# A hybrid layer's head loop with TensorE's order written by hand, and the step-size columns joined to the values' product

## The chip, the cores and the metric

The kernel runs on one core of one Trainium2 chip. The metric is device time in microseconds of one execution. The kernel before took 1650.42 us, the median of 3 runs (1649.81 to 1650.58).

## The reference, cut to what matters

A transformer block (pooled mixer with sparse attention, memory cross-attention, gated feed-forward) is followed by two hybrid layers over 512 tokens of width 1024. Only the hybrid layers are touched. One of them computes, from its input `x`:

```
proj = x @ w_in            # q, k, v, z_attn, z_ssm, xbc, dt_raw (16 columns, one for each state-space head)
attn = sliding_window_attention(q, k, v, sinks) * silu(z_attn)
xs, B, C = split(silu(causal_depthwise_conv(xbc)))         # 1024 + 256 + 256 channels
dt = softplus(dt_raw + dt_bias);  a = -exp(a_log)
y  = ssd_chunked(xs, dt, a, B, C) + xs * d_skip            # 4 chunks of 128 tokens
ssm = gated_rmsnorm(y, z_ssm)
out = layer_norm(alpha * x + concat(attn, ssm) @ w_out)
```

In `ssd_chunked`, with `a_cs` the running sum of `dt * a` inside a chunk, the diagonal part of a head is `(C B^T * exp(a_cs[l] - a_cs[s]) for l >= s) @ (xs * dt)`. The off-diagonal part multiplies `C` by a state that is carried from chunk to chunk and scales with `exp(a_cs[l])`.

## The kernel before, in words

Activations lie transposed: 128 channels on the partitions, 512 tokens along the free axis. A projection of 128 output channels is a *unit*: 1024 x 128 weights, loaded by one DMA into `wraw` and split into a rounded part `whi` (ScalarE, line 107) and the rest `wlo` (VectorE, two halves, line 110). The layer's input `h` is split in the same way. `mm3` (lines 147 to 154) then issues 24 matmuls of 512 columns: for each of 8 blocks `whi*xh` and `whi*xl`, then 8 times `wlo*xh`. There are three buffers each of `wraw`, `whi` and `wlo`. PSUM has 4 banks with the tag `mm` (units), 2 with `lg` and 2 with `tr`. Large tiles of 128 x 512 come from two pools of 34, `G` and `R`, and small ones from `ht`, `sq` and `rs` of two each.

SyncE's queue runs in the order of the program text. On the other engines a planner orders instructions at build time, by the text's order as priority and by its own estimate of when each could start. Once built, every engine runs its list in order.

One hybrid layer (`hybrid`) does this, in text order:

1. Four gate units (`z_ssm`), block by block over the two halves of the tokens (`units_by_k`, lines 174 to 177).
2. `dt`: 16 matmuls with a 48-column stationary tile, the columns of the high and the low part (line 931). Then the units of B and C with their convolution (`conv`, lines 895 to 906: one ScalarE operation, three on VectorE, tanh, one more on VectorE). The softplus, the scan over tokens and the exponentials of `dt` run on 16 partitions x 512 (lines 932 to 953). `a_cs` and its exponential go to DRAM; eight transposes (lines 959, 960) bring `dt` and `a_cs` to token order.
3. Convolution units 0 and 1, the products `C B^T` (line 979), units 2, 3 and 4.
4. `tokens(0)`: for each chunk four transposes (line 1007), two multiplications on VectorE (lines 1010, 1014) and the state's matmul (line 1016), whose result is added to the carried state (lines 1021, 1022).
5. The loop over eight pairs of heads. Step j issues one more unit (convolutions 5 to 7, then gates 4 to 7), `decay(j + 1)` and `heads(j)`; step 3 also issues `tokens(1)`. `decay` turns rows of `a_cs`, fetched from DRAM by broadcast, into weights: four clamped differences of 128 x 128 for each head, the exponential, and a product with `C B^T` on GpSimd or VectorE. The clamps run on ScalarE as a Relu (line 1057), or, for the first head of the pair from pair 3 on, on VectorE (line 1055). `heads` issues 16 matmuls (line 1070) and 6 (line 1076), and three VectorE operations (lines 1078 to 1080). Then the gate is multiplied in (line 1110) and squares are summed. Step 6 also issues the first half's norm (`gated_norm`, line 1087).
6. After the loop: the two key units; the values' product, 96 matmuls of 256 columns with `h` as the stationary operand (lines 1139 to 1141); the second half's norm; 16 heads of attention with the remaining query and gate units between them; the output projection with its tail.

Of the kernel before, what the change touches and what calls it, by code (L numbers as in the profile page):

```python
# [61 lines left out]
class Kern:  # L62
# [79 lines left out]
    def mm3(self, out, w, xs, m=P, start=True, stop=True, woff=0):  # L142

        nc = self.nc
        whi, wlo = w
        n = len(xs)
        for k, (xh, xl) in enumerate(xs):
            c = slice(woff + k * m, woff + (k + 1) * m)
            nc.tensor.matmul(out, whi[:, c], xh, start=start and k == 0, stop=False)  # L149
            nc.tensor.matmul(out, whi[:, c], xl, start=False, stop=False)  # L150
        self.begin()
        for k, (xh, xl) in enumerate(xs):
            c = slice(woff + k * m, woff + (k + 1) * m)
            nc.tensor.matmul(out, wlo[:, c], xh, start=False, stop=stop and k == n - 1)  # L154

# [719 lines left out]
    def l2_consts(self):  # L875
# [4 lines left out]
        self.small = self.load("small16", [16, 4], nc.sync)  # L880

    def hybrid(self, L):
# [4 lines left out]
        e16 = lambda: self.f("G")[:16, :]  # L887
        xr, e, uu, sm, dtf, acs, seg = (e16() for _ in range(7))
        nc.scalar.dma_start(seg, a["segs"])

# [4 lines left out]
        def conv(j, tag, w=None):  # L895

            y, o = self.f("ht"), self.f(tag)
            cw = lambda w: cwh[:, w * 12 + j : w * 12 + j + 1]
            pt = self.proj(W[4 + j], h, w=w)
# [14 lines left out]
        wd = self.s("w256", (P, 256), 9)[:, :P]  # L914
        nc.sync.dma_start(wd, a["w_dt"][L])
        wdt = self.s("wdt", (P, 48 * KD), 1, F32R)
        nc.gpsimd.memset(wdt.bitcast(F32), 0.0)
        w3, wd3 = wdt.rearrange("p (k m) -> p k m", m=48), wd.rearrange("p (k m) -> p k m", m=16)
        self.split(wd3, w3[:, :, :16], w3[:, :, 32:])

# [11 lines left out]
        nc.scalar.activation(xr, pt[32:48], AF.Identity, bias=self.small[:, L : L + 1])  # L932
        nc.vector.tensor_tensor(xr, pt[:16], xr, ALU.add)
        BC = [conv(8 + j, "R") for j in range(4)]
# [9 lines left out]
        nc.vector.scalar_tensor_tensor(dtf, xr, 0.0, uu, ALU.max, ALU.add)  # L944
        av = self.s("av", (16, 1), 2)
        nc.scalar.activation(av, self.small[:, 2 + L : 3 + L], AF.Exp)
        nc.vector.tensor_scalar(av, av, -1.0, None, ALU.mult)
        nc.vector.tensor_scalar(e, dtf, av, None, ALU.mult)
        nc.vector.tensor_tensor_scan(acs, seg, e, 0.0, ALU.mult, ALU.add)
        self.acsd = self.dp.tile([2, 16, S], F32, tag=f"acs{L}", name=f"acs{L}")  # L950
        nc.scalar.dma_start(self.acsd[0], acs)
        nc.scalar.activation(seg, acs, AF.Exp)
        nc.scalar.dma_start(self.acsd[1], seg)
        B, C = BC[:2], BC[2:]

        ptd = self.ps("tr")
        for c in range(4):
            cc = slice(c * P, (c + 1) * P)
            nc.tensor.transpose(ptd[:, c * 16 : c * 16 + 16], dtf[:, cc], self.ident[:16, :16])
            nc.tensor.transpose(ptd[:, 64 + c * 16 : 80 + c * 16], acs[:, cc], self.ident[:16, :16])  # L960
        dtt = self.s("dtt", (P, 128))
        nc.vector.tensor_copy(dtt, ptd[:, :128])
        dtok, atok = dtt[:, :64], dtt[:, 64:]
# [7 lines left out]
        nc.vector.tensor_tensor(dend, dend, dtok, ALU.mult)  # L971
        xs = [conv(0, "G"), conv(1, "G")]
# [28 lines left out]
        def tokens(g):  # L1001

            for c in range(4):
                cc = slice(c * P, (c + 1) * P)
                ptx = self.ps("tr")
                for j in range(4):
                    nc.tensor.transpose(ptx[:, j * P : (j + 1) * P], xs[4 * g + j][:, cc], self.ident)
                xdt[g, c] = self.f("G")
                o = c * 16 + 8 * g
                nc.vector.tensor_tensor(d3(xdt[g, c]), d3(ptx), bc(dtok, o), ALU.mult)  # L1010
                if c == 3:
                    break
                xe = self.f("ht")
                nc.vector.tensor_tensor(d3(xe), d3(ptx), bc(dend, o), ALU.mult)
                pst = self.ps("lg")
                nc.tensor.matmul(pst, bt[c][:, g * P : (g + 1) * P], xe, start=True, stop=True)
                prev = self.f("R")
                if c == 0:
                    nc.scalar.copy(prev, pst)
                else:  # L1020
                    nc.vector.tensor_tensor(d3(prev), d3(prevs[g, c - 1]), bc(cdec, o), ALU.mult)
                    nc.vector.tensor_tensor(prev, prev, pst, ALU.add)
                prevs[g, c] = prev

        def decay_rows(j):

            dfs, ee = [self.f("R") for _ in range(2)], self.f("R")
            for e_, df in enumerate(dfs):
                row = self.acsd[:, 2 * j + e_, :]
                nc.sync.dma_start(df, row[:1].broadcast_to([P, S]))  # L1030
                nc.sync.dma_start(ee[64 * e_ : 64 * e_ + 64, P:], row[1:, P:].broadcast_to([64, S - P]))
            return dfs, ee

        for j in range(2, 4):
            xs.append(conv(j, "G"))
        xs.append(conv(4, "G"))

        fill = [9, 10, 11, 28, 29, 30, 31]
        wn = self.weights(W[fill[0]])
        rows = [decay_rows(0), decay_rows(1)]  # L1040
        tokens(0)

        def decay(j):

            dfs, ee = rows.pop(0)
            if j < 6:
                rows.append(decay_rows(j + 2))
            for e_, df in enumerate(dfs):
                hd = 2 * j + e_
                cut = e_ == 0 and j >= 3  # L1050
                for c in range(4):
                    cc = slice(c * P, (c + 1) * P)
                    at = atok[:, c * 16 + hd : c * 16 + hd + 1]
                    if cut:
                        nc.vector.tensor_scalar(df[:, cc], df[:, cc], at, 0.0, ALU.subtract, ALU.min)
                    else:
                        nc.scalar.activation(df[:, cc], df[:, cc], AF.Relu, bias=at, scale=-1.0)
                nc.scalar.activation(df, df, AF.Exp, scale=1.0 if cut else -1.0)
# [31 lines left out]

        cat = [None] * 16
        accs = []
        ws = decay(0)
        for j in range(8):
            g = j // 4
            w = wn
            if j < 6:
                wn = self.weights(W[fill[j + 1]])
            if j < 3:
                xs.append(conv(5 + j, "G", w))  # L1100
            elif j < 7:
                zs.append(self.f("R"))
                silu(zs[-1], self.proj(None, h, w=w))
            nxt = decay(j + 1) if j < 7 else None
            if j == 3:
                tokens(1)
            heads(j, *ws)
# [321 lines left out]
```

## Time and profile before

| | |
|---|---|
| median of 3 runs | 1650.42 us (1649.81 to 1650.58) |
| the profiled execution's own time | 1650.6 us |
| its span, first to last instruction | 1648.8 us |
| busy: TensorE, VectorE, ScalarE, GpSimd | 97%, 69%, 49%, 13% of the span |
| mean granted TensorE clock | 0.994 of 2.4 GHz |

Times of stretches are microseconds from the span's start. The first hybrid layer's part that is touched goes from its gate units (about 836) to the start of attention (about 1010), the second's from about 1243 to about 1420. A matmul's duration in the rows runs from its start to the modelled arrival of its last result, so neighbours overlap; from one start to the next is what it costs the engine. "PE" is the matmuls, "PEld" the loading of the stationary operand, DVE is VectorE, ACT is ScalarE, POOL is GpSimd.

### The profile page before, as it was taken

How to read it: one execution, taken by the hardware profiler on the slowest of the kernel's cores; microseconds unless marked ns; L12 is line 12 of the kernel's file. 1: busy time of each engine (PE TensorE's matmuls, PEld its weight loads, DVE VectorE, ACT ScalarE, POOL GpSimd, SP SyncE). 2: the span in 40 equal slices, each digit the busy share in tenths (PEclk: the TensorE clock that was granted, in tenths of full speed). 3: DMA queues.
4: the chain of work that ended last, by engine and by line, in shares of the span. 5: the costliest groups of instructions: out<-in, count | busy, mean ns of one | idle time of the engine just before them, and what ended most of it. 6: DMA issues, size and time to landing. Idle time of an engine off the chain costs nothing. (4 is left out here: it accounts for less than half of the span.)

```text
span 1648.8 us, 24498 instructions
## 1 busy us (share of the span) xinstructions
PE 1601.2 (97%) x9014; PEld 1358.7 (82%) x9014; DVE 1140.7 (69%) x2490; ACT 805.5 (49%) x1571; POOL 212.4 (13%) x251
## 2 busy tenths in 40 slices
PE   8999999999999999999999999999999989999996
PEld 5778888889898888888998778887998867888786
DVE  6779967547886455533767998765497799777447
ACT  4543245336863333323556556665355555666424
POOL 2000213000100000000000121211230022111131
PEclk9999999999999999999999999999999999999998
DMA  6522332243233323234636223211452522322133
GB/s 222 198 97 76 120 103 64 77 158 116 81 116 111 102 92 100 89 104 119 196 124 191 80 77 103 78 65 51 141 171 81 178 87 78 102 78 65 64 103 116
DMA packets 66233, 180.28 MB, mean 109 GB/s; under 512 B 7953, under 2 KB 19169, under 8 KB 66113
## 3 DMA queue, kind: packets, MB, share of 16 engines
q1 hardware_dynamic: 56320, 166.75, 31.8%
q10 hardware_dynamic: 9792, 11.96, 2.4%
q8 instruction: 71, 1.16, 0.3%
q14 instruction: 50, 0.40, 0.1%
HBM read 170.14 MB, written 9.06 MB: 109 GB/s over the span
## 5 line engine op out<-in xcount | busy, mean ns | idle before, releaser
L149 PE MATMUL psmm<-G,whi 128*128 128x512 f32 (+2 forms) x1244 | 479.2, 388 | 2.2 <-ACT whi L107 2.2
L110 DVE TENSOR_TENSOR wlo<-wraw,whi 128x512 fp32r<-128x512 f32 x515 | 358.8, 718 | 174.8 <-ACT whi L107 123.8
L150 PE MATMUL psmm<-G,whi 128*128 128x512 f32 (+2 forms) x1244 | 473.6, 384 | 0.0
L107 ACT CAST whi<-wraw 128x1024 fp32r<-128x1024 f32 (+3 forms) x262 | 267.7, 1024 | 339.7 <-PE psmm L150 272.3
L154 PE MATMUL psmm<-G,wlo 128*128 128x512 f32 (+2 forms) x1244 | 299.5, 382 | 0.0
L149 PEld LDWEIGHTS psmm<-G,whi 128*128 128x128 f32 (+1 forms) x1244 | 233.3, 188 | 50.3 <-issue 3.5
L150 PEld LDWEIGHTS psmm<-G,whi 128*128 128x128 f32 (+1 forms) x1244 | 233.2, 188 | 45.3 <-issue 1.5
L154 PEld LDWEIGHTS psmm<-G,wlo 128*128 128x128 f32 (+1 forms) x1244 | 228.2, 187 | 45.0
L149 PE MATMUL psmm<-R,whi 128*128 128x256 f32 (+1 forms) x684 | 210.4, 329 | 0.0
L150 PE MATMUL psmm<-R,whi 128*128 128x256 f32 (+1 forms) x684 | 210.1, 328 | 0.0
L149 PEld LDWEIGHTS psmm<-R,whi 128*128 128x128 f32 x684 | 130.0, 190 | 11.8 <-issue 0.3
L150 PEld LDWEIGHTS psmm<-R,whi 128*128 128x128 f32 x684 | 130.0, 190 | 11.5
L154 PE MATMUL psmm<-R,wlo 128*128 128x256 f32 (+1 forms) x684 | 130.3, 329 | 0.0
L154 PEld LDWEIGHTS psmm<-R,wlo 128*128 128x128 f32 x684 | 106.2, 190 | 11.5
L200 POOL TENSOR_TENSOR acc<-acc,sq 128x512 f32<-128x512 f32 (+1 forms) x42 | 53.0, 1261 | 475.4 <-ACT sq L199 475.3
L1176 ACT ACTIVATE w<-w,st 128x256 f32<-128x256 f32 (+1 forms) x128 | 59.9, 470 | 29.3 <-DVE st L1174 29.3
L211 ACT ACTIVATE sq<-ht 128x512 f32<-128x512 f32 (+1 forms) x48 | 29.4, 613 | 60.8 <-DVE ht L902 30.0
L902 DVE SCALAR_TENSOR_TENSOR ht<-psmm,cwh,ht 128x511 f32<-128x511 f32 (+2 forms) x72 | 53.4, 742 | 5.8 <-ACT ht L900 4.6
L836 DVE TENSOR_TENSOR sq<-psmm,G 128x512 f32<-128x512 f32 (+1 forms) x24 | 15.5, 646 | 56.0 <-PE psmm L154 56.0
L1172 DVE CUSTOM_DVE_ANT_0 w<-pslg,w,sinks 128x256 f32<-128x256 f32 (+1 forms) x128 | 51.5, 444 | 1.1 <-PE pslg L1167 0.6
L199 ACT ACTIVATE sq<-G 128x256 f32<-128x256 f32 (+1 forms) x76 | 35.1, 463 | 34.3 <-DVE G L1264 25.9
L1181 POOL TENSOR_SCALAR w<-w,st 128x256 f32<-128x256 f32 x64 | 37.9, 604 | 86.8 <-DVE st L1179 79.0
(332 smaller groups left out, 2597.3 us busy)
## 6 DMA issues: line engine op xcount, KB each, us to landing
wraw<-w_in SPq DMA_DIRECT2D x112, 512.0 KB, 3.4
wraw<-w_out SPq DMA_DIRECT2D x56, 512.0 KB, 3.8
wraw<-w_down SPq DMA_DIRECT2D x24, 512.0 KB, 3.5
wraw<-w_gate SPq DMA_DIRECT2D x22, 512.0 KB, 3.4
wraw<-w_up SPq DMA_DIRECT2D x22, 512.0 KB, 3.4
R<-acs SPq DMA_DIRECT2D x32, 256.0 KB, 5.7
wraw<-w_down SPq DMA_DIRECT2D x12, 384.0 KB, 3.7
wraw<-w_proj_attn SPq DMA_DIRECT2D x8, 512.0 KB, 3.4
```

The lines of the kernel that those rows point to most:

```text
L107: nc.scalar.copy(hi[:, :n], raw[:, :n])
L110: nc.vector.tensor_tensor(lo[:, c], raw[:, c], hi[:, c].bitcast(F32), ALU.subtract)
L149: nc.tensor.matmul(out, whi[:, c], xh, start=start and k == 0, stop=False)
L150: nc.tensor.matmul(out, whi[:, c], xl, start=False, stop=False)
L154: nc.tensor.matmul(out, wlo[:, c], xh, start=False, stop=stop and k == n - 1)
L199: self.last_sq = nc.scalar.activation(t, src, AF.Square)
L200: (eng or nc.gpsimd).tensor_tensor(acc, acc, t, ALU.add)
L211: self.last_tanh = self.nc.scalar.activation(out, src, AF.Tanh, scale=scale)
L902: nc.vector.scalar_tensor_tensor(y[:, s:], pt[:, : S - s], cw(3 - s), y[:, s:], ALU.mult, ALU.add)
L1172: nc.vector.tensor_tensor_reduce(pr, pt, al[:, 256 - n :], 1.0, sink, ALU.add, ALU.max, mx[:, b : b + 1])
L1176: nc.scalar.activation(prs[b], prs[b], AF.Exp, bias=nm[:, b : b + 1], accum_out=sm[:, b : b + 1])
L1181: (nc.gpsimd if b % 2 else nc.vector).tensor_scalar(prs[b], prs[b], rc[:, b : b + 1], 1.0, ALU.mult, ALU.mult)
```

## The change

The `dt` columns are appended to the values' weights (272 columns), and this product moves to the place of the `dt` product, with four `mm` banks. Its values go to two tiles of the pool `R` (they were in `G`). `dt` now comes out with tokens on the partitions, so the softplus chain works on 128 x 64, and the running sum is a matmul with a triangular matrix. `a_cs` goes to DRAM as 64 rows of 128. B's and C's units come after this chain in the text. All clamps run on ScalarE. The loop becomes one block in which TensorE's instructions keep the text's order: nine units (convolutions 4 to 7, gates 4 to 7, the first key unit) are cut into single matmuls, 216 in all, and dealt out between the transposes, states and heads. `tokens` is split into `tokens(g, c)` and `state(g, c)`, and the scaled copies `xe` use the tag `rs` instead of `ht`.

```diff
+    def unit(self, w, xs):
+        whi, wlo = w
+        pt = self.ps()
+        def products():
+            n = len(xs)
+            for p in range(3 * n):
+                k = p // 2 if p < 2 * n else p - 2 * n
+                c = slice(k * P, (k + 1) * P)
+                lhs, rhs = (whi, xs[k][p % 2]) if p < 2 * n else (wlo, xs[k][0])
+                self.nc.tensor.matmul(pt, lhs[:, c], rhs, start=p == 0, stop=p == 3 * n - 1)
+                yield
+        return pt, products()
...
-        pt = self.ps("lg")[:48]
-        for k in range(KD):
-            for n, x in enumerate(h[k]):
-                nc.tensor.matmul(pt, wdt[:, 48 * k : 48 * k + 48], x, start=k + n == 0, stop=k == 7 and n == 1)
+        vs = [self.f("R") for _ in range(2)]
+        pv = [self.ps() for _ in range(4)]
+        for c in range(3):
+            n = min(3, KD - 3 * c)
+            wh, wl = self.weights(a["w_vdt"][L][:, 816 * c : 816 * c + 272 * n], 272 * n)
+            for t, pt in enumerate(pv):
+                o, tt = pt[:, :272], slice(t * P, (t + 1) * P)
+                for kk in range(n):
+                    k = 3 * c + kk
+                    ws = slice(272 * kk, 272 * kk + 272)
+                    nc.tensor.matmul(o, h[k][0][:, tt], wh[:, ws], start=k == 0, stop=False)
+                    nc.tensor.matmul(o, h[k][0][:, tt], wl[:, ws], start=False, stop=False)
+                    nc.tensor.matmul(o, h[k][1][:, tt], wh[:, ws], start=False, stop=k == 7)
...
+        for t, pt in enumerate(pv):
+            nc.vector.tensor_tensor(xr[:, 16 * t : 16 * t + 16], pt[:, 256:272], self.dtb[:, hb], ALU.add)
+            nc.scalar.copy(vs[t // 2][:, 256 * (t % 2) : 256 * (t % 2) + 256], pt[:, :256])
...
+        pa = self.ps("tr")
+        nc.tensor.matmul(pa[:, :64], self.tril, e, start=True, stop=True)
+        nc.vector.tensor_copy(atok, pa[:, :64])
+        prow = self.ps("tr")
+        nc.tensor.transpose(prow[:64, :P], atok, self.ident)
...
+        BC = [conv(8 + j, "R") for j in range(4)]
...
-                    if cut:
-                        nc.vector.tensor_scalar(df[:, cc], df[:, cc], at, 0.0, ALU.subtract, ALU.min)
-                    else:
-                        nc.scalar.activation(df[:, cc], df[:, cc], AF.Relu, bias=at, scale=-1.0)
+                    nc.scalar.activation(df[:, cc], df[:, cc], AF.Relu, bias=at, scale=-1.0)
...
+        def step(j):
+            if j < 7:
+                ws.append(decay(j + 1))
+            heads(j, *ws.pop(0))
+            if j < 5:
+                rows.append(decay_rows(j + 3))
...
+        with self.tc.manual_schedule(engines={mybir.EngineType.PE}):
+            for g, lead in ((0, 20), (1, 20)):
+                feed(lead)
+                tokens(g, 0)
+                tokens(g, 1)
+                feed(10 - 2 * g)
+                state(g, 0)
+                tokens(g, 2)
+                feed(6)
+                state(g, 1)
+                tokens(g, 3)
+                feed(8 - 2 * g)
+                state(g, 2)
+                if g == 0:
+                    for n, j in ((8, 0), (24, 1), (22, 2)):
+                        feed(n)
+                        step(j)
+                else:
+                    for n, j in ((0, 3), (10, 4), (22, 5), (22, 6), (22, 7)):
+                        feed(n)
+                        step(j)
+                    feed(2)
+        keys(self.proj(W[1], h))
```

## Rows read from the trace of the kernel before

**Rows 1.** The page: the engines' busy time, then TensorE's busy tenths in 40 slices of the span.

```profile
PE 1601.2 (97%) x9014; PEld 1358.7 (82%) x9014; DVE 1140.7 (69%) x2490; ACT 805.5 (49%) x1571; POOL 212.4 (13%) x251
...
PE   8999999999999999999999999999999989999996
```

**Rows 2.** Busy time by stretch: length, then each engine's busy microseconds (with the number of instructions), the granted clock as a share of 2.4 GHz, the DMA engines' busy share and GB/s. In the first hybrid layer: from the `dt` product to the first transposes of `tokens(0)`, from there to the values' product, that product, the start of attention, attention; then the second layer's stretch from its `tokens(0)` to its values' product.

```profile
854.60:910.90 56.30, 56.30 (x266) 45.67 (x266) 44.55 (x72) 34.98 (x62) 3.01 (x3) 1.00 0.59 172
910.90:993.60 82.70, 75.84 (x440) 58.18 (x439) 77.43 (x130) 44.13 (x81) 20.34 (x13) 1.00 0.26 79
993.60:1005.20 11.60, 11.60 (x98) 11.60 (x97) 7.13 (x12) 4.97 (x7) 0.00 (x0) 1.00 0.60 166
1005.20:1020.00 14.80, 14.45 (x69) 11.22 (x68) 12.86 (x25) 9.61 (x14) 0.00 (x0) 1.00 0.19 66
1020.00:1100.00 80.00, 80.00 (x461) 66.69 (x461) 59.40 (x182) 54.58 (x150) 17.46 (x32) 1.00 0.22 73
...
1315.50:1398.00 82.50, 76.00 (x441) 58.33 (x440) 77.55 (x128) 43.44 (x80) 19.15 (x13) 1.00 0.25 77
```

**Rows 3.** Who TensorE waited for between 836 and 1010: microseconds in total, times, the longest.

```profile
PE pslg L1016 <- DVE ht L1014: 3.1, 2, 1.9
PE pstr L1007 <- DVE G L905: 1.6, 1, 1.6
PE pstr L1070 <- DVE G L1078: 1.2, 2, 0.9
...
PE pstr L206 <- DVE G L1078: 0.5, 1, 0.5
```

**Rows 4.** TensorE in order of time (start, microseconds, engine, line): the `dt` product and the matmul that follows it; the first two of the eight small transposes; eight matmuls of a unit.

```profile
854.65 3.87 PE L931 MATMUL pslg<-G,wdt 128*48 128x512 f32 x16
...
858.36 0.39 PE L149 MATMUL psmm<-G,whi 128*128 128x512 f32 x1
...
880.24 0.23 PE L959 MATMUL pstr<-ident,G 16*128 16x16 f32 x1
880.32 0.21 PE L960 MATMUL pstr<-ident,G 16*128 16x16 f32 x1
...
991.74 1.98 PE L154 MATMUL psmm<-G,wlo 128*128 128x512 f32 x8
```

**Rows 5.** Groups of matmuls, shapes kept apart (count, busy microseconds, mean nanoseconds of one): the values' product, and one line that has a shape of 384 columns.

```profile
L1139 PE MATMUL psmm<-whi,G 128*128 128x256 f32 x64 | 18.1, 283 | 0.0
...
L594 PE MATMUL psmm<-G,G 128*128 128x384 f32 x8 | 2.7, 339 | 0.0
```

**Rows 6.** The end of the gate units in order of time, on ScalarE and VectorE: the next weights' split, and a gate's two operations between the halves of `wlo`.

```profile
853.65 1.05 ACT L107 CAST whi<-wraw 128x1024 fp32r<-128x1024 f32 x1 [7.47 <-PE psmm L176]
...
854.73 0.69 DVE L110 TENSOR_TENSOR wlo<-wraw,whi 128x512 fp32r<-128x512 f32 x1 [8.10 <-PE psmm L176]
...
855.34 0.74 DVE L911 SCALAR_TENSOR_TENSOR R<-R,psmm 128x256 f32<-128x256 f32 x2
856.00 0.68 DVE L110 TENSOR_TENSOR wlo<-wraw,whi 128x512 fp32r<-128x512 f32 x1
```

**Rows 7.** The softplus chain in order of time: the table load ahead of the logarithm and the logarithm; later, a small operation of 128 x 64.

```profile
863.28 1.28 ACT L940 ACT_TABLE_LOAD   x1
...
864.58 0.63 ACT L940 ACTIVATE G<-G 16x512 f32<-16x512 f32 x1
...
882.41 0.21 DVE L969 TENSOR_TENSOR dend<-pstr,dtt 128x64 f32<-128x64 f32 x1
```

**Rows 8.** TensorE in the loop, in order of time: a state's two passes and the transposes behind them, then one pair's 16 and 6 matmuls and what follows.

```profile
917.04 1.06 PE L1016 MATMUL pslg<-ht,G 128*128 128x512 f32 x2
917.94 0.49 PE L1007 MATMUL pstr<-ident,G 128*128 128x128 f32 x3
...
958.81 1.09 PE L1070 MATMUL pstr<-R,G 128*64 128x128 f32 x16
...
960.52 2.09 PE L154 MATMUL psmm<-G,wlo 128*128 128x512 f32 x8
```

**Rows 9.** VectorE in the loop, in order of time: two operations of a chunk's tokens, then a convolution's and a pair's.

```profile
920.51 0.68 DVE L1010 TENSOR_TENSOR G<-pstr,dtt 128x512 f32<-128x512 f32 x1
921.11 0.68 DVE L1014 TENSOR_TENSOR ht<-pstr,dend 128x512 f32<-128x512 f32 x1
...
923.67 0.74 DVE L902 SCALAR_TENSOR_TENSOR ht<-psmm,cwh,ht 128x511 f32<-128x511 f32 x1
924.34 0.74 DVE L1078 SCALAR_TENSOR_TENSOR G<-G,vecs,pstr 128x512 f32<-128x512 f32 x1
```

**Rows 10.** GpSimd's product and a clamp on VectorE in order of time, and an ordinary clamp shortly before them.

```profile
935.22 0.28 DVE L1055 TENSOR_SCALAR R<-R,dtt 128x128 f32<-128x128 f32 x1
...
936.18 1.30 POOL L1059 TENSOR_TENSOR R<-R,R 128x512 f32<-128x512 f32 x1 [12.06 <-ACT R L1058]
936.28 1.28 DVE L1055 TENSOR_SCALAR R<-R,dtt 128x128 f32<-128x128 f32 x1
```

**Rows 11.** The clamps between 919 and 1000, by line (count, busy microseconds, mean nanoseconds): on VectorE, and on ScalarE.

```profile
L1055 DVE TENSOR_SCALAR R<-R,dtt 128x128 f32<-128x128 f32 x20 | 8.3, 439 | 0.0
...
L1057 ACT ACTIVATE R<-R,dtt 128x128 f32<-128x128 f32 x28 | 9.2, 389 | 0.0
```

**Rows 12.** DMA issues: count, KB each, median microseconds from issue to landing.

```profile
R<-acs SPq DMA_DIRECT2D x32, 256.0 KB, 5.7
```

More of the change, by code (lines that the diff above doesn't have):

```diff
@@ L943, in hybrid @@
         nc.vector.tensor_tensor(uu, uu, sm, ALU.add)
[L944 to L963, printed above, removed]
+        nc.vector.scalar_tensor_tensor(dtok, xr, 0.0, uu, ALU.max, ALU.add)
+        av = self.s("av", (P, 16), 2)
+        nc.scalar.activation(av, self.alog[:, hb], AF.Exp)
+        d4 = lambda t: t.rearrange("p (c h) -> p c h", h=16)
+        nc.vector.scalar_tensor_tensor(d4(e), d4(dtok), -1.0, av.unsqueeze(1).broadcast_to([P, 4, 16]), ALU.mult, ALU.mult)
+        pa = self.ps("tr")
[3 more added lines that the diff above has]
+        nc.tensor.transpose(prow[:64, :P], atok, self.ident)
+        ar, er = self.s("ar", (64, P)), self.s("er", (64, P))
+        nc.scalar.copy(ar, prow[:64, :P])
+        nc.scalar.activation(er, prow[:64, :P], AF.Exp)
+        self.acsd = self.dp.tile([2, 64, P], F32, tag=f"acs{L}", name=f"acs{L}")
+        nc.scalar.dma_start(self.acsd[0], ar)
+        nc.scalar.dma_start(self.acsd[1], er)
         pl = self.ps("tr")
@@ L999, in hybrid, with tokens @@
         prevs = {}
[L1001 to L1019, printed above, removed]
-                else:
-                    nc.vector.tensor_tensor(d3(prev), d3(prevs[g, c - 1]), bc(cdec, o), ALU.mult)
-                    nc.vector.tensor_tensor(prev, prev, pst, ALU.add)
-                prevs[g, c] = prev
+        def tokens(g, c):
+            cc = slice(c * P, (c + 1) * P)
+            ptx = self.ps("tr")
+            for j in range(4):
+                nc.tensor.transpose(ptx[:, j * P : (j + 1) * P], xs[4 * g + j][:, cc], self.ident)
+            xdt[g, c] = self.f("G")
+            o = c * 16 + 8 * g
+            nc.vector.tensor_tensor(d3(xdt[g, c]), d3(ptx), bc(dtok, o), ALU.mult)
+            if c < 3:
+                xe[c] = self.f("rs")
+                nc.vector.tensor_tensor(d3(xe[c]), d3(ptx), bc(dend, o), ALU.mult)
@@ new lines, in state @@
+        def state(g, c):
+            o = c * 16 + 8 * g
+            pst = self.ps("lg")
+            nc.tensor.matmul(pst, bt[c][:, g * P : (g + 1) * P], xe.pop(c), start=True, stop=True)
+            prev = self.f("R")
+            if c == 0:
+                nc.scalar.copy(prev, pst)
+            else:
+                nc.vector.tensor_tensor(d3(prev), d3(prevs[g, c - 1]), bc(cdec, o), ALU.mult)
+                nc.vector.tensor_tensor(prev, prev, pst, ALU.add)
+            prevs[g, c] = prev
@@ L1088, in gated_norm, with gate_evict, stream, feed @@
                 cat[8 + i] = self.pair(t, "R")
+        fill = [8, 9, 10, 11, 28, 29, 30, 31, 0]
+        evict = [lambda pt, j=j: xs.append(conv(j, "G", pt)) for j in range(4, 8)]
+        def gate_evict(pt):
+            zs.append(self.f("R"))
+            silu(zs[-1], pt)
+        evict += 4 * [gate_evict] + [lambda pt: keys(pt)]
+        ahead = []
+        def stream():
+            for u, e in enumerate(evict):
+                pt, products = self.unit(ahead.pop(0), h)
+                if fill:
+                    ahead.append(self.weights(W[fill.pop(0)]))
+                for i, _ in enumerate(products):
+                    if i == 3 * KD - 1:
+                        e(pt)
+                    yield
+        fillers = stream()
+        def feed(n):
+            for _ in range(n):
+                next(fillers)
         cat = [None] * 16
         accs = []
[L1093 to L1107, printed above, removed]
-            ws = nxt
+        ws = []
+        def step(j):
[4 more added lines that the diff above has]
+                rows.append(decay_rows(j + 3))
             y = xs[j]
@@ L1127, in hybrid @@
             kt.append(ks)
[L1128 to L1143 removed]
+        xe = {}
+        rows = [decay_rows(0)]
+        for j in range(2, 4):
+            xs.append(conv(j, "G"))
+        ahead.append(self.weights(W[fill.pop(0)]))
+        rows += [decay_rows(1), decay_rows(2)]
+        ws.append(decay(0))
+        with self.tc.manual_schedule(engines={mybir.EngineType.PE}):
[15 more added lines that the diff above has]
+                        step(j)
+                else:
+                    for n, j in ((0, 3), (10, 4), (22, 5), (22, 6), (22, 7)):
[3 more added lines that the diff above has]
+        keys(self.proj(W[1], h))
         gated_norm(1, accs[1])
```

75 lines of the change are left out of this document (20 added, 55 removed).

## The prediction, made before the change was run

> **What bounds the kernel now.** I read the page first. TensorE is busy 97% of the span and in nearly every slice [rows 1], so time can come from two places only: TensorE's own work, and the few microseconds in which it stands idle. Next I asked for busy time by stretch [rows 2]. In the first hybrid layer TensorE is busy without a break up to `tokens(0)`, during the values' product and, but for 0.35 us, in attention. The idle time lies in the head loop: 82.70 - 75.84 = 6.86 us there and 82.50 - 76.00 = 6.50 us in the second layer. In the same stretch VectorE is busy 77.43 of 82.70 us. So the loop is a place where VectorE runs nearly full beside TensorE, and TensorE catches up with it now and then. The waits say where [rows 3]: the states wait for the scaled copy (3.1 us in 2 waits), the transposes for a convolution's last operation (1.6), the next pair for a `tr` bank that line 1078 has not yet emptied (1.2), the norm likewise (0.5). All four end at VectorE. What follows is worked out for one layer against the profiled execution, 1650.6 us, which is 0.2 us above the median, so no correction is made.
>
> **TensorE's own work.** The `dt` product goes: from 854.65 to the next matmul at 858.36, 3.71 us [rows 4]. Its 16 matmuls stream all 512 tokens for 48 columns of weights. The eight small transposes start some 0.07 us apart [rows 4]: 0.5 us goes. In exchange 96 matmuls of the values grow from 256 to 272 columns. No row has that width. The bounds are the durations at 256 and 384 columns, 283 and 339 ns [rows 5]: between 0 and 56 ns each, 0 to 5.4 us. I take the straight line between them, 16 x 56 / 128 = 7 ns each, 0.7 us, because 272 is next to 256. The triangular matmul and the transpose of the sums add some 0.25 us (three small ones like those of [rows 4]). Sum: -3.7 - 0.5 + 0.7 + 0.25 = -3.3 us for a layer. It counts fully, since TensorE is busy all through this stretch.
>
> **The new product's start.** The `dt` matmuls had their weights ready long before, and for 3.7 us they covered the split of the next unit. The values' product stands there without a cover. Its three `whi` buffers are free only when the gate units end: the cast starts at 853.65 and ends at 854.70, and of `wlo` the first half comes at 854.73 to 855.42, the second, behind two gate operations, at 856.00 to 856.68 [rows 6]. The new chunk has 816 columns, so its cast ends some 0.2 us earlier. But its second matmul already reads `wlo`, and its fourth reads columns 272 to 544, which lie in both halves. TensorE, free at 854.65, waits until 855.2 at best and 856.5 if the gate operations come in between. Less than 0.6 us needs a better order than the row's, and 2.0 us is the whole split. I take 1.2. Behind the waiting matmul stands all of TensorE's list, which has nothing else to do here. The later two chunks have 36 matmuls each in front of them, over 4 us, against about 2 us of split.
>
> **The chain.** Twelve operations of 128 x 64 (0.21 us on VectorE) and a table load of 1.28 us before the logarithm [rows 7] give about 12 x 0.3 + 1.3 = 5 us, an estimate from these rows. It lies beside B's first unit, 24 x 0.227 = 5.4 us ((1.98 - 0.39) / 7 for one matmul [rows 4]), with three more behind that. What isn't hidden is a wrong guess of the planner: three small matmuls stand in TensorE's list where it thought the chain would be done. Bounds: 0, and 1.9 us, the longest wait in [rows 3]. I take 0.4. On the logarithm, the row has the table load's 1.28 us and the operation right behind it. The Trainium skill ("ScalarE: Activation LUTs", What ACT_TABLE_LOAD costs) counts a further 1380 ns of drain for a switch, about 2.66 us in all. By the page the chain would be 1.4 us longer, and if the planner missed it, the wait would be 1.8 and the whole some 3 us later. The row has no such gap.
>
> **The loop.** TensorE's demand in the new order: 9 units x 5.45 = 49.0 us; 32 transposes of about 0.11, 3.5; six states of 0.9 (917.04 to 917.94), 5.4; eight pairs of 1.71 (958.81 to 960.52), 13.7 [rows 8]; the norm's matmul, two passes like a state's, 0.9. Together 72.5 us. VectorE's operations start 0.60 apart, those with three operands 0.67 [rows 9]. Counted so: four convolutions at 3.8 with the weights' `wlo`, 15.2; four gates at 1.8, 7.2; the key unit 2.4; the pairs at 2.8 with `decay`'s product and the gate, 21.8; tokens and states 6.6 for each half, 13.2; the norm 6.9; what convolution 3 leaves over, 2.6. That is 69.3 us. To this come GpSimd's spells: one clamp started 0.10 us behind a product on GpSimd and ended with it, 1.28 us in place of 0.28 [rows 10]. With five such spells (an estimate; GpSimd has 13 operations there [rows 2]) it is 74 us. The two engines are level, so the lists decide. Up to pair 4 TensorE needs 49.3 us and VectorE, by the same counts, 47.7 + 3 + 0.8 for the start = 51.5: about 2.2 us of idle. After that a step has 22 matmuls and a pair, 6.7 us, against 4.6 on VectorE, and only the norm's bank wait (0.5, [rows 3]) remains. The 20 leading matmuls (4.5 us) just cover the last convolution before each `tokens` (0.8 + 2.0 + 0.6 + 0.6 us). So the idle falls from 6.7 us (mean) to about 2.5. Bounds: 0.5, and the 6.7 of now.
>
> Taking the 20 clamps off VectorE spares 20 x 0.20 us (the mean of 439 ns holds some that ran into GpSimd) and all of it lies behind pair 2, where VectorE recovers anyway. The Trainium skill ("GPSIMD Engine Reference", Specifications) says why such a spell stays: GpSimd shares its SBUF interfaces with VectorE, and operations with two SBUF inputs contend too. By that rule the next `wlo` or product waits where the clamp did, and the gain is 4 us and not 20 x 0.36 = 7.2; [rows 10] show the wait itself. On ScalarE the clamps add 20 x 0.29 = 5.9 us [rows 11], hidden beside 44.13 of 82.70 us busy [rows 2]. With no cover they would cost up to 1.2 us ahead of each of pairs 3 to 7. The row fetches, now in pieces of 512 bytes, are issued after a pair for the one three later. Two steps are 13 us, and a fetch takes 5.7 [rows 12]. SyncE's queue has the next unit's weights behind them; I cost this at nothing.
>
> **After the loop.** The values' product was 11.6 us of TensorE with 7.13 of VectorE [rows 2], a cover of 4.5 us just before attention, where VectorE is then busy 12.86 of 14.80. Now one key unit and the queries follow at once, while VectorE has the last pair, two key splits and the second norm (2.2 + 4.8 + 6.9 us). Queries 0 and 1, the key unit and a gate give TensorE 21.8 us; VectorE's load up to the first softmax is some 23. Bounds 0 and 4.5 us; I take 0.6.
>
> **Sum.** -3.3 + 1.2 + 0.4 + (2.5 - 6.7) + 0.6 = -5.3 us for a layer, -10.6 for both: 1640 us, with a range of its own of 1635 to 1645.
>
> **Rivals.** (a) The covers hold everywhere: loop 0.5, start 0.6, the rest 0. -3.3 + 0.6 - 6.2 = -8.9, so 1633 us. For it: the waits of now come from pairs and states placed back to back. Against: VectorE's 74 us. (b) VectorE sets the loop whatever TensorE's order: the 6.7 us stay, and -3.3 + 2.2 = -1.1 gives 1648. For it: VectorE's 94% [rows 2]. (c) Slower: the hand-written order turns lateness into waiting. The loop has 22 places where TensorE must have VectorE's result (8 chunks, 6 states, 8 pairs), the units behind each can't move up, and a late unit delays its own convolution, on which the next place waits. The waits of now are 6.4 us in 6 places, about 1.0 each [rows 3]. At 15 of the 22 places that is 15 us: -3.3 + 8.3 + 2.2 = +7.2 for a layer, 1665 us. It decides from 9.4 us of idle, 0.43 at each place, where the gain is gone and 0.2% lost. Against it: VectorE has the time, on average. (d) A matmul of 272 columns costs like one of 384: 4.7 us more for a layer, 1649 us; against it the even growth in [rows 5].
>
> **Numbers.** Chances: forecast 0.42, (a) 0.20, (b) 0.20, (c) 0.12, (d) 0.06. A measurement tells 0.2%, 3.3 us, from no change: faster is below 1647.1. That holds the forecast, (a) and about a third of (b): 0.70. The rest of (b) and (d) is the same, 0.17, and (c) slower with a little of (d), 0.13. Range 1630 to 1651: it leaves out (c) and the outer end of (a).
>
> **What would show it.** Starts of the 272-column matmuls 0.12 to 0.13 us apart, not 0.15 or more; a break of about 1 us in TensorE behind the gate units; loop waits of about 0.5 us each at pairs 3 and 4 and at the second half's states, and hardly any at pairs 5 to 7; VectorE above 90% up to pair 4. Wrong if the loop's idle passes 7 us, or if attention begins with a wait of several microseconds.

## The result and the profile after

The changed kernel takes 1667.8 us, the median of 4 runs (1664.66 to 1670.56), against 1650.12 us for the kernel before on the same chip: a ratio of 1.0107, 95% interval 1.0085 to 1.0129. It is slower by about 1%. The forecast was 1640 us with 1630 to 1651 as its range, so both the sign and the range were wrong.

The page of the profiled execution (1670.56 us, mean granted clock 0.985), busy time and TensorE's tenths:

```profile
PE 1604.8 (96%) x8972; PEld 1361.0 (82%) x8972; DVE 1115.0 (67%) x2454; ACT 812.0 (49%) x1615; POOL 210.1 (13%) x249
...
PE   8999999999899999999998999999999899999996
```

Beside [rows 1] TensorE has 42 instructions fewer and yet 3.6 us more busy time. More time for fewer matmuls suggests that the clock fell somewhere. I compared the part from the end of the gate units to the first attention score, layer by layer. The first layer's windows, first of the kernel before, then of the changed one (columns as in [rows 2]):

```profile
854.53:1013.75 159.22, 152.36 (x837) 121.97 (x836) 135.80 (x223) 90.33 (x159) 23.34 (x16) 1.00 0.40 120
```

```profile
856.55:1024.47 167.92, 154.27 (x823) 124.45 (x821) 121.88 (x203) 93.45 (x179) 21.80 (x15) 0.96 0.44 117
```

The second layer's are 158.90 and 167.82 us. The layers lost 8.7 and 8.9 us here, together 17.6 of the 20.0 us between the two profiled executions (the medians differ by 17.7). TensorE's idle time rose from 6.86 to 13.65 us, and the granted clock fell from 1.00 to 0.96. VectorE, which the prediction put level with TensorE in the loop, has 14 us less to do. Who TensorE waited for, between 840 and 1030 (in the second layer the same seven waits come again):

```profile
PE psmm L149 <- ACT whi L107: 4.6, 1, 4.6
PE pstr L222 <- POOL acc L216: 3.1, 1, 3.1
PE pstr L1010 <- ACT G L1014: 2.9, 1, 2.9
PE pstr L222 <- DVE G L1086: 1.2, 1, 1.2
PE pstr L1026 <- DVE G L919: 1.2, 1, 1.2
PE pslg L1038 <- DVE rs L1032: 0.4, 1, 0.4
PE psmm L947 <- DVE wlo L110: 0.2, 1, 0.2
```

The last four answer to [rows 3] and to the new product's start: 3.0 us, less than the prediction allowed. The first three are new, and none ends at VectorE. They lie ahead of the loop and behind it. The stretches around them, by windows:

```profile
904.60:918.50 13.90, 6.35 (x18) 4.68 (x17) 7.34 (x13) 11.63 (x29) 2.55 (x2) 0.63 0.53 96
...
925.20:1003.80 78.60, 75.82 (x444) 58.85 (x443) 66.92 (x107) 45.47 (x90) 14.22 (x10) 1.00 0.43 110
...
1009.80:1018.00 8.20, 5.08 (x14) 3.43 (x13) 5.63 (x9) 2.46 (x5) 3.73 (x2) 0.79 0.61 153
```

Read the idle time (length less TensorE's busy time) and the clock together: 7.55 us idle at 904.6 with a clock of 0.63, and 3.12 us idle at 1009.8 with 0.79. The loop between them idles 2.78 us at full clock. In order of time, TensorE at the first break, then ScalarE there:

```profile
907.78 0.44 PE L1010 MATMUL pstr<-ident,R 128*128 128x128 f32 x2 [2.92 <-ACT G L1014]
912.84 0.79 PE L149 MATMUL psmm<-G,whi 128*128 128x512 f32 x1 [4.62 <-ACT whi L107]
913.43 0.63 PE L150 MATMUL psmm<-G,whi 128*128 128x512 f32 x1
913.86 0.63 PE L149 MATMUL psmm<-G,whi 128*128 128x512 f32 x1
```

```profile
906.84 0.63 ACT L227 ACTIVATE sq<-ht 128x512 f32<-128x512 f32 x1 [3.39 <-DVE ht L916]
907.37 0.63 ACT L1014 COPY G<-pstr 128x256 f32<-128x256 f32 x2
...
911.23 0.63 ACT L1066 ACTIVATE R<-R 128x512 f32<-128x512 f32 x1
911.76 2.92 ACT L107 CAST whi<-wraw 128x1024 fp32r<-128x1024 f32 x3
```

Behind the break matmuls of 512 columns start 0.43 us apart and not 0.23, until 918.1: the granted clock is 0.50 there, the 1.2 GHz level. Behind the second break they start 0.43 us apart as well, from 1014.74 to 1017.30. On ScalarE the copies (line 1014) stand behind convolution 1's tanh (line 227). The cast of the weights of convolution unit 2, the first of the three casts in the last line, stands behind all of pair 0's clamps and exponentials (lines 1065, 1066), and starts without idle time ahead of it: it waited for its turn. The DMA issues between 850 and 1010 (count, KB each, median us from issue to landing) offer another culprit; the first fence is the changed kernel, the second the kernel before:

```profile
wraw<-w_in SPq DMA_DIRECT2D x22, 512.0 KB, 8.0
R<-acs SPq DMA_DIRECT2D x16, 256.0 KB, 12.8
R<-acs SPq DMA_DIRECT2D x16, 96.0 KB, 11.9
```

```profile
wraw<-w_in SPq DMA_DIRECT2D x23, 512.0 KB, 3.5
R<-acs SPq DMA_DIRECT2D x16, 256.0 KB, 5.5
```

So two theories stood for the first break: the 512-byte pieces of the row fetches (the pieces theory), or the order of ScalarE's list, in which pair 0's clamps come ahead of the casts (the list theory). For the second break one name stood: GpSimd's last addition of squares, 3.32 us long.

### The profile page after: what moved, and what is told of

Same layout as the page of the kernel before. It is cut to its first block, busy times and chain, and to the rows that moved or that the text cites. A ratio compares the mean times of both kernels' runs of the same rounds, so it can differ in the third digit from the quotient of the medians.

```text
span 1668.5 us, 24417 instructions
## 1 busy us (share of the span) xinstructions
PE 1604.8 (96%) x8972; PEld 1361.0 (82%) x8972; DVE 1115.0 (67%) x2454; ACT 812.0 (49%) x1615; POOL 210.1 (13%) x249
## 5 line engine op out<-in xcount | busy, mean ns | idle before, releaser
L110 DVE TENSOR_TENSOR wlo<-wraw,whi 128x512 fp32r<-128x512 f32 (+1 forms) x519 | 356.5, 709 | 185.3 <-ACT whi L107 158.4
L107 ACT CAST whi<-wraw 128x1024 fp32r<-128x1024 f32 (+4 forms) x264 | 268.0, 1018 | 349.4 <-PE psmm L150 252.0
L149 PE MATMUL psmm<-G,whi 128*128 128x512 f32 (+2 forms) x1100 | 426.9, 391 | 10.2 <-ACT whi L107 10.2
L150 PE MATMUL psmm<-G,whi 128*128 128x512 f32 (+2 forms) x1100 | 421.7, 387 | 0.0
L154 PE MATMUL psmm<-G,wlo 128*128 128x512 f32 (+2 forms) x1100 | 264.0, 381 | 0.0
L149 PEld LDWEIGHTS psmm<-G,whi 128*128 128x128 f32 (+1 forms) x1100 | 209.1, 190 | 54.4 <-ACT whi L107 11.0
L150 PEld LDWEIGHTS psmm<-G,whi 128*128 128x128 f32 (+1 forms) x1100 | 209.5, 191 | 41.4 <-issue 1.8
L154 PEld LDWEIGHTS psmm<-G,wlo 128*128 128x128 f32 (+1 forms) x1100 | 201.1, 187 | 39.2
L150 PEld LDWEIGHTS psmm<-R,whi 128*128 128x128 f32 x684 | 130.1, 190 | 11.5
L154 PEld LDWEIGHTS psmm<-R,wlo 128*128 128x128 f32 x684 | 106.2, 190 | 11.5
L167 PE MATMUL psmm<-G,whi 128*128 128x512 f32 x288 | 74.2, 399 | 0.0
L916 DVE SCALAR_TENSOR_TENSOR ht<-psmm,cwh,ht 128x511 f32<-128x511 f32 (+2 forms) x72 | 53.7, 745 | 18.5 <-ACT ht L914 17.6
L167 PEld LDWEIGHTS psmm<-G,whi 128*128 128x128 f32 x288 | 52.8, 188 | 11.3 <-issue 1.0
L1067 POOL TENSOR_TENSOR R<-R,R 128x512 f32<-128x512 f32 x16 | 21.7, 1354 | 260.0 <-ACT R L1066 260.0
```

Source lines behind the costliest of these rows:

```text
L107: nc.scalar.copy(hi[:, :n], raw[:, :n])
L110: nc.vector.tensor_tensor(lo[:, c], raw[:, c], hi[:, c].bitcast(F32), ALU.subtract)
L167: self.nc.tensor.matmul(pt, lhs[:, c], rhs, start=p == 0, stop=p == 3 * n - 1)
L916: nc.vector.scalar_tensor_tensor(y[:, s:], pt[:, : S - s], cw(3 - s), y[:, s:], ALU.mult, ALU.add)
L1067: (nc.vector if e_ else nc.gpsimd).tensor_tensor(df, df, cb[hd // 8], ALU.mult)
```

## The experiments

All start from the changed kernel unless the kernel before is named. Stretch times are again from the end of the gate units to the first score, first layer then second (changed kernel 167.92 and 167.82 us, before 159.22 and 158.90).

**Whole rows (e1).** `a_cs` stored so that a head's row is 2 KB in one piece.

```diff
-        nc.tensor.transpose(prow[:64, :P], atok, self.ident)
+        nc.vector.tensor_copy(at4.rearrange("p (h c) -> p c h", c=4), d4(pa[:, :64]))
+        nc.tensor.transpose(prow[:64, :P], at4, self.ident)
...
+                nc.sync.dma_start(df, row[:1].broadcast_to([P, S]))
```

> The changed kernel with the running sums stored so that a head's row is 2 KB in one piece again (the transposed tile has its columns in the order head, chunk; one small VectorE copy more); nothing else moves, and on every engine the order of the list stays. Two theories for the 8.8 us that each layer lost. Pieces: the row fetches in 512-byte pieces (12.8 us to land, 5.7 before) hold up the unit weights behind them and so cause the stall ahead of the loop; then the two breaks of 2.9 and 4.6 us and the half clock after them (2.9 us) go: about 10 us per layer, 1647 to 1652 us. List: in the trace the weights of units 6 to 8 are in SBUF some 12 us before their cast runs, and the cast waits because it stands in ScalarE's list behind pair 0's clamps and exponentials; then landing sooner changes nothing there, the breaks stay at 2.9 and 4.6 us, and the time is 1662 to 1668 us. I hold the list likelier.

Measured: 1667.14 us, ratio to before 1.0101 (1.0077 to 1.0125). The fetches land in 4.9 and 5.0 us, the weights in 3.8, and the breaks are the same 2.9 and 4.6 us. ScalarE's list has the same order, the three casts behind the clamps and exponentials, again without idle time ahead of them:

```profile
906.71 0.63 ACT L1069 ACTIVATE R<-R 128x512 f32<-128x512 f32 x1
907.25 2.92 ACT L107 CAST whi<-wraw 128x1024 fp32r<-128x1024 f32 x3
```

The pieces alone are not the cause; the list theory held its first test.

**Rows fetched later (e2).**

```diff
-        rows = [decay_rows(0)]
         for j in range(2, 4):
             xs.append(conv(j, "G"))
         ahead.append(self.weights(W[fill.pop(0)]))
-        rows += [decay_rows(1), decay_rows(2)]
+        rows = [decay_rows(j) for j in range(3)]
```

> The changed kernel with one line moved in the text: pair 0's rows are fetched behind convolution units 2 and 3 and the first filler's weights, not ahead of them. The 512-byte pieces stay. List: the casts of these three units then stand ahead of pair 0's clamps in ScalarE's list, the 4.6 us break goes with most of the half clock behind it (2.9 us); the 2.9 us break may go or stay: 7 to 10 us per layer, 1648 to 1654 us. Pieces: the fetches are as slow as before, and now pair 0's rows come later still, so the loop's first decay starts late and the loop waits: 1665 us or more.

Measured: 1666.62 us, ratio 1.0108 (1.0071 to 1.0145). Both breaks ahead of the loop are gone, as the list theory said, but a wait of 9.9 us (8.0 in the second layer) came in their place, and the time stayed. TensorE's longest wait, and ScalarE's list in order of time:

```profile
PE pstr L1026 <- DVE G L919: 9.9, 1, 9.9
```

```profile
915.42 0.39 ACT L1065 ACTIVATE R<-R,atok 128x128 f32<-128x128 f32 x1
924.70 1.04 ACT L107 CAST whi<-wraw 128x1024 fp32r<-128x1024 f32 x1 [8.89 <-DMA wraw<-w_in]
...
927.49 0.61 ACT L227 ACTIVATE sq<-ht 128x512 f32<-128x512 f32 x1
```

ScalarE stands 8.89 us at the cast of the next filler's weights, which have not landed; behind it in the list is convolution 3's tanh (927.49), on which `tokens(0)` waits. The weights are late because SyncE issues them behind the row pieces, of which six in a row hold its queue from 895.57 to 908.98, 0.7 to 4.5 us each:

```profile
895.57 4.53 SPq L1053 DMA_DIRECT2D R<-acs  x1
...
909.08 8.61 SPq L104 DMA_DIRECT2D wraw<-w_in  x3
```

Neither theory was right as stated. These two runs suggest two causes, one behind the other, each enough by itself; e5 tests that.

**The norm's last addition on VectorE (e3).**

```diff
-            self.sumsq(y, accs[-1], j % 4 == 0)
+            self.sumsq(y, accs[-1], j % 4 == 0, nc.vector if j == 7 else None)
```

> The changed kernel with the last of the eight additions of squares on VectorE instead of GpSimd; nothing else. The second break of each layer (3.1 us ahead of the norm's sum over the partitions, then 2.4 us of half clock) ends with GpSimd's addition of 3.3 us. If that addition is its cause, an addition of some 0.6 us on VectorE in its place takes about 2.7 us of the break and up to 2.4 us of the half clock away: 3 to 5 us per layer, 1658 to 1662 us. Rival: the square on ScalarE and the gate product ahead of it are just as late, VectorE has a queue of its own there, and the break stays near 3 us: 1666 to 1668 us.

Measured: 1659.3 us, ratio 1.0055 (1.0036 to 1.0074), 8.5 us less than the changed kernel. The stretches are 163.32 and 162.94 us, 4.6 and 4.9 less; the wait fell from 3.1 to 0.2 us, so some 1.8 of each layer's gain is the clock that no longer falls.

**Pieces in the kernel before (e4).**

```diff
+        cut4 = lambda i: self.acsd[i].rearrange("(c h) l -> h c l", h=16)
+        nc.scalar.dma_start(cut4(0), acs.rearrange("h (c l) -> h c l", l=P))
...
+                nc.sync.dma_start(df.rearrange("p (c l) -> p c l", l=P), rows_of(0, hd, 0, P))
```

> The kernel before, with its running sums stored as 64 rows of 128 and fetched in 512-byte pieces as the changed kernel does; the order of all lists as before. It prices the pieces alone. Pieces theory: landings of some 12 us instead of 5 push pair 0's decay and the weights behind the fetches late, and the time rises by 5 us or more, to 1655 us and above. List theory: the fetches stand two pairs ahead and the weights have 8 us in hand, so the time stays within 2 us of 1650.

Measured: 1658.22 us, ratio 1.0046 (1.0029 to 1.0063). The fetches land in 11.9 and 11.5 us, and the stretches are 161.73 and 163.58 us, 2.5 and 4.7 longer. The pieces cost time with the old order too; the list theory's "within 2 us" was wrong.

**Both row edits (e5): e1 and e2 together.**

> Whole rows of 2 KB and pair 0's rows behind the three weight fetches, both edits in one kernel; the norm's last addition stays on GpSimd. Alone, neither moved the time: with whole rows the casts still stood behind pair 0's clamps; with the fetches moved, the breaks of 2.9 and 4.6 us went, but one of 9.9 us came at the loop's first transposes, where ScalarE's next cast waits for weights that lie behind the row pieces in SyncE's queue. Theory: two causes one behind the other, each enough; then both edits together take 7 to 10 us per layer away, and the time is 1646 to 1653 us, with less than 3 us of breaks between the gate units and the loop's first transposes. Rival: ScalarE and VectorE have too much to do there whatever the order and the fetches, and a break of 7 us or more shows up in a third place: 1660 us or more.

Measured: 1646.45 us, ratio 0.9973 (0.9961 to 0.9985). Of the four corners (1667.8 neither, 1667.14 whole rows, 1666.62 later rows, 1646.45 both) only the last moves, by 21 us. So the two causes do stand one behind the other. The stretches are 157.42 and 157.47 us. Of TensorE's waits in the first layer the norm's is left, and ahead of the loop only this one at its first transposes:

```profile
PE pstr L222 <- POOL acc L216: 3.1, 1, 3.1
...
PE pstr L1028 <- DVE G L919: 1.1, 1, 1.1
```

**All three (e6): e5 with e3's addition.**

> Both row edits and the last square's addition on VectorE. If the three causes are all that was missed, the addition takes the same 8 us here as it took alone, and what is left is the change as the prediction had it: 1638 to 1645 us, below the kernel before. Rival: with the first break gone the end of the loop comes when ScalarE or a transfer is not ready, and part of the 8 us stays: 1646 to 1652 us, no faster than before.

Measured: 1636.72 us, ratio 0.9912 (0.9897 to 0.9927): faster than the kernel before. This is the change as the prediction had imagined it, and its first layer's window prices the steps (the second is 152.89 us long):

```profile
854.66:1007.54 152.88, 149.58 (x822) 121.42 (x821) 120.48 (x204) 92.83 (x179) 18.82 (x14) 1.00 0.43 128
```

Beside the changed kernel, TensorE's busy time is 154.27 - 149.58 = 4.7 us less with the same matmuls (one record fewer): that is what the half clock cost in each layer.

**The clamps alone in the kernel before (e7).**

```diff
-                cut = e_ == 0 and j >= 3
+                cut = False
```

> The kernel before with its five clamps per layer that stood on VectorE (even heads of pairs 3 to 7) moved to ScalarE, alone. 20 tensor_scalars per layer go from VectorE, 20 activations of 0.33 us come on ScalarE, 6.6 us per layer. If VectorE's lateness makes the loop's waits of before (the ones on the tokens' products and on the gate product), they shorten: 1645 to 1649 us. If the waits come from the order alone, nothing moves: 1649 to 1652 us. If ScalarE in the list's order becomes late with its casts: 1653 us or more.

Measured: 1645.86 us, ratio 0.9975 (0.9963 to 0.9987), by the medians 4.8 us less than the kernel before. The transposes' wait of 1.6 us [rows 3] is gone from both layers. The first layer's stretch is shorter by that (157.65 us). The second's is unchanged, because TensorE is busy 1.6 us longer there than the 152.40 us of the kernel before, at a granted clock of 0.99:

```profile
1253.84:1412.70 158.86, 153.97 (x837) 123.11 (x835) 131.46 (x202) 95.74 (x179) 23.42 (x15) 0.99 0.40 120
```

The first layer of e11, where no wait is longer than in the kernel before, has such a dip too (busy 153.88 us at 0.99), so it isn't put down to the clamps. The waits, then, show 3.2 of the 4.8 us. The rest can't be placed: the end of the first layer's gate units, with the same code ahead of it, lies anywhere from 851.6 to 856.6 us in these profiles.

**The clamps back on VectorE, with all three edits (e8).** The branch of the kernel before put into e6.

> All three edits, and the even heads' clamps of pairs 3 to 7 back on VectorE, as the kernel before had them. Prices the clamps in the hand-written order. Prediction's working: ScalarE has the room, and VectorE is the busier; then this is 1 to 4 us slower than all three edits with the clamps on ScalarE. Rival: VectorE has the time beside TensorE's fillers too, and the two are within 1 us.

Measured: 1638.76 us, ratio 0.9930 (0.9910 to 0.9950), 2.0 us more than e6. The stretches are 153.57 and 153.56 us, 0.7 more each. The 20 clamps take 278 ns on average here; none ran into GpSimd, as some did in [rows 10, 11].

**The planner's order in the loop, with all three edits (e9).**

```diff
-        with self.tc.manual_schedule(engines={mybir.EngineType.PE}):
+        if True:
```

> All three edits, and TensorE's order in the head loop left to the planner again: the same text without the line that keeps the written order. It prices the hand-written order by itself. Prediction's working: of the loop's 6.7 us of waits in the kernel before, the order took some 4 away, so the planner's order costs 3 to 5 us per layer: 1642 to 1647 us. Rival: the waits went because of the smaller steps in the text (a chunk of tokens, a state, a pair with fillers between) and the clamps on ScalarE, and the planner keeps them apart as well: 1635 to 1639 us.

Measured: 1629.21 us, ratio 0.9864 (0.9848 to 0.9881). So the hand-written order costs 7.5 us beside the planner's, which neither expectation had allowed. The first layer's window (the second is 150.44 us long) and its waits:

```profile
851.61:1002.02 150.41, 149.67 (x824) 121.66 (x823) 121.80 (x204) 92.87 (x180) 17.95 (x14) 1.00 0.42 130
```

```profile
PE pstr L222 <- DVE acc L216: 0.3, 1, 0.3
...
PE psmm L947 <- DVE wlo L110: 0.2, 1, 0.2
PE pstr L1028 <- DVE G L919: 0.2, 1, 0.2
```

The same matmuls, the same busy time, and 0.74 us idle where e6 has 3.30. From the first score to the last, attention takes 112.7 us in e9 and 113.9 in e6, which is another 1.2 for each layer. Some 0.5 of that is the wait of attention's first transposes for GpSimd (0.8 us in e6, 0.3 in e9); the rest is open. e9 is the fastest version.

**Other portions of fillers in the written order (e10).** Six matmuls more ahead of the first `tokens`, six fewer ahead of pair 1, and the first norm eight matmuls later.

```diff
-            for g, lead in ((0, 20), (1, 20)):
+            for g, lead in ((0, 26), (1, 20)):
...
-                    for n, j in ((8, 0), (24, 1), (22, 2)):
+                    for n, j in ((8, 0), (18, 1), (22, 2)):
```

> All three edits, and the two longest waits left in the loop covered: six filler matmuls more ahead of the first tokens (taken from ahead of pair 1), and the first norm eight filler matmuls later. Of 1.1 and 1.2 us per layer some 0.8 each should go: 1632 to 1635 us. Rival: pair 1 now waits for its products, or the norm's later results delay the second half's squares and the last norm, and the time stays at 1636 to 1638 us.

Measured: 1641.85 us, ratio 0.9940 (0.9923 to 0.9957), a miss in the other direction. Both waits went, and one of 4.5 us at the first state came. VectorE in order of time shows why:

```profile
924.26 0.69 DVE L919 SCALAR_TENSOR_TENSOR G<-sq,ht 128x512 f32<-128x512 f32 x1 [0.70 <-ACT sq L227]
924.87 0.68 DVE L1031 TENSOR_TENSOR G<-pstr,dtok 128x512 f32<-128x512 f32 x1
925.47 0.68 DVE L1034 TENSOR_TENSOR rs<-pstr,dend 128x512 f32<-128x512 f32 x1
```

A unit has 24 matmuls. With 26 ahead of `tokens`, convolution 4's VectorE work (up to line 919) comes ahead of the tokens' products (lines 1031, 1034) in VectorE's list, and the state waits for all of it.

**A control (e11): e3's edit in the kernel before.**

> A control: the kernel before with the last addition of squares on VectorE. There the values' product, 11.6 us of TensorE, stands between the loop and the norm's matmul, and GpSimd's addition (2.88 us in the trace of before) is over before it ends. So the edit that took 8 us off the changed kernel should do nothing here: 1649 to 1652 us. Rival: GpSimd's addition also slows VectorE's operations beside it, and it matters in both: 1644 to 1647 us.

Measured: 1650.81 us, ratio 0.9992 (0.9982 to 1.0001): nothing. Where the values' product follows the loop, the addition is hidden, as far as the interval can tell.

**The planner's order alone (e12): e9's edit in the changed kernel.**

> The changed kernel with one line less: TensorE's order in the head loop left to the planner; row pieces, row order and GpSimd's addition as they are. Last question: is the hand-written order what made the change slower? With the three edits the planner's order was worth 7.5 us in all. If the causes add up, the same comes off here, 1658 to 1662 us, and the breaks ahead of the loop (2.9 and 4.6 us) and the norm's (3.1 us) stay, because the order of ScalarE's list and GpSimd's addition don't hang on that line. Rival: the planner also puts other work into these breaks, the change is no slower than before, 1645 to 1653 us, and then the hand-written order is the cause after all.

Measured: 1661.7 us, ratio 1.0069 (1.0049 to 1.0089), 6 us less than the changed kernel. The first layer still waits 3.5, 2.9 and 2.7 us in the three places. The stretches show less of the 6 us: 164.88 and 168.54 us, 3.0 shorter in the first layer and 0.7 longer in the second, where the granted clock is 0.95. So the written order is a cause by itself, beside the others, and not the main one, and part of its price lies outside these stretches.

## Why the prediction was wrong

**The row fetches: the step that failed most.** "SyncE's queue has the next unit's weights behind them; I cost this at nothing." I took 5.7 us for a fetch from [rows 12], measured on whole rows of 2 KB, for fetches in pieces of 512 bytes; they took 12.8. And I asked only whether the rows would be in time for their pair, not what the moved fetch did to the order of ScalarE's list. Fetch and list together cost 10.4 us for each layer (e5), of which 7.5 are breaks and the rest is the clock behind them (TensorE's busy time is 154.27 us in the changed kernel and 151.20 in e5).

**After the loop: right place, wrong engine and size.** I named the values' product as a cover of 11.6 us that goes away, and took 0.6 us out of 0 to 4.5, from VectorE's load alone. What is late next is GpSimd's addition. It cost 4.6 to 4.9 us for each layer (e3), clock included, where the cover is gone and nothing measurable where it stands (e11).

**The clock: a term I did not have.** [rows 2] shows 1.00 in all stretches, and I priced each wait at its own length. Here the 7.55 us of idle time ahead of the loop and the 3.12 behind it were each followed by matmuls at the 1.2 GHz level, which cost 4.7 us for each layer (e6 against the changed kernel).

**TensorE's own work: right.** -3.3 predicted; 152.36 to 149.58 in e6 is -2.8. The 272-column matmuls start 0.125 us apart (12 of them from 867.72 to 869.09), those of 256 columns 0.120. 96 x 0.0045 = 0.4 us, where I had 0.7; rival (d) falls.

**The start and the chain: too dear.** 1.2 and 0.4 us predicted, 0.2 and 0 measured. No gate operation came ahead of the first half of `wlo`, which began at 856.57 with the gates' last matmul. In the chain the changed kernel has two table loads, and the activation follows 1.29 us after the load's start:

```profile
871.24 1.28 ACT L961 ACT_TABLE_LOAD   x1
872.53 0.26 ACT L961 ACTIVATE uu<-uu 128x64 f32<-128x64 f32 x1
```

The Trainium skill ("ScalarE: Activation LUTs", What ACT_TABLE_LOAD costs) would have a further 1380 ns between them; this trace again has none, and TensorE waited at no small matmul.

**The loop: right in size, wrong about its source.** 2.5 us predicted, 2.8 measured, with no wait at pairs 3 and 4 and 1.2 us each ahead of the first tokens and at the norm's bank. But I credited the written order with it. The planner, given the same text, leaves hardly any (e9), so the gain over the kernel before comes from something other than that order. I have no run with only the smaller steps in the kernel before, so their share was not tried. The clamps, to which the prediction gave nothing, are worth 0.7 us a layer in the new order (e8) and a wait of 1.6 us in the old one (e7).

**The rivals.** (c) named 1665 us and a written order that waits. The time is near, for another reason: the loop waits in 3 places, not 15, and the loss lies outside it. Its mechanism is real but smaller: 7.5 us in all (e6 to e9), and e10 shows it at one place. (b) falls too: VectorE is busy 66.92 of 78.60 us in the loop, not 77 of 83. Up to pair 4 (925.2 to 978) it is busy 46.34 of 52.80 us, 88%, just under the 90% named as a sign. (a), covers that hold everywhere, comes only in e9, with the planner's order and all three edits. Of my two signs of being wrong, the loop's idle past 7 us did not come. A wait of several microseconds close ahead of attention did, 3.1 us.

## What to carry to other kernels

A moved or reshaped transfer is priced at its new shape, and then followed into every in-order list behind it: the DMA queue, and the engine whose cast waits for the next transfer. When a stage that covered something is moved away, list all engines that finish under that cover, not only the busiest. Two causes in series hide each other, so edits that do nothing alone are tried together before either theory is dropped; and an order written by hand is compared with the planner's on the same text before it is kept.

## What the runs showed of the hardware

**Row fetches in 512-byte pieces.** The same 256 KB broadcast took 12.8 us in pieces of 512 bytes and 4.9 us in pieces of 2 KB (e1), and 512 KB of weights on the same queue 8.0 and 3.8 (but 4.4 in e2 and e4, which have the pieces too). The Trainium skill ("DMA: Bandwidth & Descriptors", Specifications) names 512 B as the smallest transfer that still reaches line rate; here, for these broadcast rows, a fetch at that size took 2.6 times as long to land as at 2 KB, and the measurement decides.

**GpSimd waits for VectorE.** The addition that takes 1.27 to 1.29 us elsewhere in the loop (once 2.15) took 3.32 at the end of it, beside three `wlo` subtractions on VectorE:

```profile
1009.88 3.32 POOL L216 TENSOR_TENSOR acc<-acc,sq 128x512 f32<-128x512 f32 x1 [8.13 <-ACT sq L215]
```

```profile
1010.20 1.87 DVE L110 TENSOR_TENSOR wlo<-wraw,whi 128x512 fp32r<-128x512 f32 x3
```

The subtractions end at 1012.07, and 1.28 us later is 1013.35, close to the addition's end at 1013.20. In e12 two subtractions stand there and not three, and the addition is 0.61 us shorter:

```profile
1005.74 2.71 POOL L216 TENSOR_TENSOR acc<-acc,sq 128x512 f32<-128x512 f32 x1 [8.13 <-ACT sq L215]
```

```profile
1006.06 1.27 DVE L110 TENSOR_TENSOR wlo<-wraw,whi 128x512 fp32r<-128x512 f32 x2
```

These subtractions end at 1007.33, 1.28 us later is 1008.61, and the addition ends at 1008.45. The prediction had only the other direction, VectorE held up by GpSimd. The Trainium skill ("SBUF — State Buffer", SBUF: two separate sides) says that GpSimd and a VectorE operation with two SBUF inputs, which these subtractions have, take a shared port pair for a whole instruction, that whoever starts first gets it, and that the other blocks. The trace agrees with the blocking. It does not show the order: in both runs the addition's record starts 0.32 us before the first subtraction, and yet the addition ends last. No run took the subtractions away.
